# A decoder block in two halves of the sequence: the first half keeps both split parts of w_in in DRAM, the second half loads them

## The chip, the cores and the metric

The kernel runs on one core of one Trainium2 chip. The metric is device time in microseconds (us) from one execution of the whole program; lower is better. All arithmetic that counts is in float32: each operand of a large product is split into two parts, a rounded one ("hi", a type that TensorE multiplies in one pass) and the rest ("lo"), and a product is made of three matmuls, hi by hi, hi by lo and lo by hi.

## The reference

One layer (DEPTH is 1) on a sequence of 2048 positions, D_MODEL 1024.

```
h = rms_norm(x, mix_norm_pre)
z = h @ w_in                      # 1024 x 2560: q, k, v (512 each), xr, gr (512 each)
attn = dilated_attention(q, k, v) # 8 heads of 64, three dilations, mixed by their log-denominators
xr = causal_depthwise_conv(xr)    # 4 taps
rec = rg_lru(xr) * gelu(gr)       # h_t = a_t * h_(t-1) + u_t along the sequence
m = concat(attn, rec) @ w_out
x = x + rms_norm(m, mix_norm_post)
h = rms_norm(x, mlp_norm_pre)
x = x + rms_norm(square(relu(h @ w_ff_in)) @ w_ff_out, mlp_norm_post)
```

The change touches only how `w_in` reaches the matmuls of `z = h @ w_in`.

## The kernel before, in words

The sequence is worked on in two halves of 1024 positions (`hf` 0 and 1), each in two blocks of 512 (`b` 0 and 1). The columns of `w_in` are cut into 20 tiles of 128 (`ct` 0 to 19): 0 to 3 are q, 4 to 7 k, 8 to 11 v, 12 to 15 the recurrent input, 16 to 19 its gate. One tile is 8 slices of 128 by 128, 512 KB in all. `product` makes the projection of one tile and one block: 8 slices by 3 matmuls, 24 matmuls into one bank of PSUM, lines L198 to L200.

`load_w` brings a tile in. It loads the raw tile in two halves (`wraw`, 256 KB each, issued on the queue of the sync engine, SP), and `split` turns each half into `wH` (a cast on ScalarE, L54) and `wL` (a subtraction, L55). The subtraction runs on GpSimd (POOL in the profile) by default; for the first tiles, and after `pj.lo = nc.vector`, on VectorE (DVE). The pool has two buffers each for `wH`, `wL` and half a raw tile. All 20 tiles are loaded and split in the first half and once more in the second half. `load_ahead` calls `load_w` one step early.

The order of the work is a written list of steps. `ORDER` is "q00 r02 q01 a0 r03 q02 a1 q03 x2 x3 a2 q10 a3", then `BETWEEN` is "r10 r11 r12 r13" and `LATER` is "q11 q12 q13". A `q` step (half, pair of heads) projects q, k and v of a pair of heads and stores their split parts to scratch in DRAM (`sq`, `sk`, `sv`); an `r` step (half, group of 128 channels) does the projections 12+c and 16+c and the recurrence (`recurrent_block`); an `a` step is the attention of one pair of heads of the first half; `x` loads a block of 512 positions. Two recurrent groups of the first half run ahead of the list, in the pool `x0`. In one `r` step the four products stand in the order recurrent input of block 0, gate of block 0, recurrent input of block 1, gate of block 1. Inside this projection stage a scheduler sets the order of the instructions on every engine from their dependencies and a model of time; on SP, too, instructions are issued one after the other, and one that waits holds up those behind it.

After every step of the list some copies from the weights to a scratch in DRAM (`swo`, `sw`) are issued on POOL's own queue, eight at a time after an `r` step of the second half (L1552). In the last steps the loads of w_out (`woL`) and the first factors of the MLP weights (`er`, stored as `sf`) are added. From then on (output projection, MLP, attention of the second half, MLP again) `w_in` is not used.

## Time and profile before

| what | value |
|---|---|
| time, median of 3 runs | 2239.87 us (2238.17 to 2241.32) |
| the profiled execution: span from its first to its last instruction (the page gives no other time for it) | 2246.4 us |
| TensorE busy / weight loads busy | 2167.4 us (96%) / 1774.6 us (79%) |
| VectorE, ScalarE, GpSimd busy | 1506.9, 1230.9, 450.9 us |
| moved by DMA | 473.51 MB, mean 211 GB/s |
| splits of w_in, both halves: casts / subtractions on GpSimd / on VectorE | 81 / 58 / 23 |

The projection stage takes the first 640 us of the span, about 0 to 300 us for the first half's tiles and 300 to 640 us for the second half's. A busy share is the part of a stretch in which an engine had an instruction running; "PEclk" is the clock that TensorE was granted, as a part of full speed; the DMA share is the mean busy share of the 16 DMA engines. POOL's DMA instructions count in its busy time.

### The profile page before, as it was taken

Reading aid. Unit: us, or ns where it says so; the run is one execution under the profiler, and the core shown is the slowest. Engines: PE = TensorE matmul, PEld = TensorE weight load, DVE = VectorE, ACT = ScalarE, POOL = GpSimd, SP = SyncE. Lnnn points to the kernel's source line nnn. Section 1 sums busy time; section 2 is a strip of 40 time slices with the busy share of each in tenths; the row PEclk is TensorE's granted clock in tenths of the full one; section 3 lists DMA queues with packets and bytes.
Section 4 is the critical chain, followed back from the end, with each engine's and each line's share of the span. In section 5 each row is a group of like instructions: output and inputs, shape, how many; then the busy total and the mean of one; then the engine's idle time right before and its main releaser. Section 6 shows DMA issues by size and latency. Waiting matters only on the chain.

```text
span 2246.4 us, 30767 instructions
## 1 busy us (share of the span) xinstructions
PE 2167.4 (96%) x10264; PEld 1774.6 (79%) x10264; DVE 1506.9 (67%) x2908; ACT 1230.9 (55%) x2489; POOL 450.9 (20%) x536
## 2 busy tenths in 40 slices
PE   8999999979999999999999999989999999999998
PEld 6678878767788788888788787778878888888887
DVE  6767465978648867675567676777766566646456
ACT  7646464655434555554666666754455555654442
POOL 5543414455223000000001111113200000000003
PEclk9999999999999999999999999999999999999999
DMA  8365684645974676878777777877553444776665
GB/s 286 100 190 176 179 242 145 183 153 163 319 255 161 221 286 242 301 265 309 223 216 221 211 237 221 234 228 225 181 189 126 169 139 164 275 236 191 193 196 179
DMA packets 224116, 473.51 MB, mean 211 GB/s; under 512 B 23428, under 2 KB 78756, under 8 KB 217684
## 3 DMA queue, kind: packets, MB, share of 16 engines
q1 hardware_dynamic: 195140, 337.52, 47.9%
q0 software_dynamic: 28816, 134.01, 16.9%
q8 instruction: 81, 1.33, 0.2%
q14 instruction: 79, 0.65, 0.1%
HBM read 337.09 MB, written 151.13 MB: 217 GB/s over the span
## 4 chain that ended last, share of the span: by engine, by line
PE 70%; DVE 10%; DMA 8%; ACT 4%; issue 3%; POOL 1%; SPq 1%; DVEq 0%; ACTq 0%; POOLq 0%
PE o L1221 8%; PE o L1222 8%; PE o L1223 8%; PE za L1072 4%; PE za L1071 4%; PE za L1073 4%; PE z L198 3%; PE z L199 3%; PE z L200 3%; PE m L858 3%; PE m L857 3%; PE m L859 3%; PE zc L1071 2%; PE zc L1072 2%; PE zc L1073 2%
## 5 line engine op out<-in xcount | busy, mean ns | idle before, releaser
L198 PE MATMUL z<-hH,wH 128*128 128x512 f32 x640 | 263.8, 412 | 15.4 <-ACT wH L54 5.7
L199 PE MATMUL z<-hL,wH 128*128 128x512 f32 x640 | 260.5, 407 | 0.3 <-DVE hL L173 0.3
L200 PE MATMUL z<-hH,wL 128*128 128x512 f32 x640 | 259.6, 407 | 0.5 <-DVE wL L55 0.5
L198 PEld LDWEIGHTS z<-hH,wH 128*128 128x128 f32 x640 | 122.9, 192 | 50.6 <-ACT wH L54 8.3
L199 PEld LDWEIGHTS z<-hL,wH 128*128 128x128 f32 x640 | 122.8, 192 | 31.2 <-issue 4.8
L200 PEld LDWEIGHTS z<-hH,wL 128*128 128x128 f32 x640 | 122.9, 192 | 30.6 <-issue 4.6
L420 ACT ACTIVATE smB<-smB,stB 128x128 f32<-128x128 f32 (+3 forms) x128 | 71.6, 560 | 90.5 <-DVE stB L414 90.2
L1076 ACT ACTIVATE sq<-sq 128x512 f32<-128x512 f32 x93 | 58.8, 632 | 92.1 <-DVE sq L1080 92.1
L55 POOL TENSOR_TENSOR wL<-wraw,wH 128x512 fp32r<-128x512 f32 x58 | 82.4, 1437 | 80.5 <-ACT wH L54 76.7
L55 DVE TENSOR_TENSOR tlB<-pT_B,thB 128x384 fp32r<-128x384 f32 x96 | 57.1, 599 | 50.4 <-ACT thB L54 47.5
L1136 POOL DMA_DIRECT2D sa<-sq x31 | 16.6, 534 | 363.9 <-ACT sq L1077 353.4
L54 ACT CAST wH<-wraw 128x512 fp32r<-128x512 f32 (+1 forms) x81 | 47.2, 612 | 65.5 <-DMA wraw<-in_dram 31.6
L420 ACT ACTIVATE sm<-sm,stA 128x256 f32<-128x256 f32 (+1 forms) x128 | 63.1, 495 | 30.3 <-DVE stA L414 29.9
L1077 ACT ACTIVATE sq<-sq 128x512 f32<-128x512 f32 x124 | 76.2, 629 | 1.8
L1255 POOL TENSOR_TENSOR y<-y,g4b 128x512 f32<-128x512 f32 x8 | 12.3, 1577 | 259.4 <-ACT junk_y L84 259.4
L414 DVE CUSTOM_DVE_ANT_0 smB<-SB,mask_b 128x128 f32<-128x128 f32 (+3 forms) x128 | 59.3, 483 | 5.7 <-PE pT_B L393 5.4
L55 DVE TENSOR_TENSOR tlA<-pT,thA 128x512 fp32r<-128x512 f32 (+1 forms) x64 | 42.4, 670 | 26.4 <-ACT thA L54 26.0
L54 ACT CAST thB<-pT_B 128x384 fp32r<-128x384 f32 x96 | 48.4, 509 | 17.8 <-PE pT_B L393 9.7
L393 PE MATMUL pT_B<-ident,smB 128*128 128x128 f32 x320 | 51.5, 276 | 2.5 <-DVE na L409 0.9
L414 DVE CUSTOM_DVE_ANT_0 sm<-S,mask_a 128x256 f32<-128x256 f32 (+1 forms) x128 | 47.5, 410 | 9.3 <-PE pT L393 4.0
L640 PE MATMUL oB<-thB,vb 128*128 128x256 f32 x192 | 46.6, 274 | 6.6 <-ACT thB L54 5.9
L1072 PE MATMUL za<-hLT,f_5H 128*128 128x512 f32 x128 | 50.0, 391 | 2.0 <-DVE hLT L55 2.0
(607 smaller groups left out, 7041.4 us busy)
## 6 DMA issues: line engine op xcount, KB each, us to landing
sa<-as POOLq DMA_DIRECT2D x31, 1024.0 KB, 6.2
w1r<-in_dram SPq DMA_DIRECT2D x56, 512.0 KB, 4.0
sa<-sq POOLq DMA_DIRECT2D x31, 768.0 KB, 4.0
wraw<-in_dram SPq DMA_DIRECT2D x79, 256.0 KB, 3.8
place<-in_dram SPq DMA_DIRECT2D x14, 1024.0 KB, 7.9
sb<-place POOLq DMA_DIRECT2D x14, 1024.0 KB, 5.3
kh<-sk SPq DMA_DIRECT2D x24, 512.0 KB, 5.0
kl<-sk SPq DMA_DIRECT2D x24, 512.0 KB, 7.1
```

The lines of the kernel that those rows point to most:

```text
L55: (lo_eng or nc.vector).tensor_tensor(out=lo, in0=src, in1=f32(hi), op=ALU.subtract))
L198: pe.matmul(z, hi[:, k, :], hh, start=(k == 0), stop=False)
L199: pe.matmul(z, hi[:, k, :], hl, start=False, stop=False)
L200: pe.matmul(z, lo[:, k, :], hh, start=False, stop=(k == KT - 1))
L414: v.tensor_tensor_reduce(out=sm[:, c0:c0 + w], in0=sp[:, c0:c0 + w], in1=mask[:, mask.shape[-1] - w:], scale=1.0, scalar=3.0e38, op0=ALU.a ...
L420: s.activation(out=sm[:, c0:c0 + w], in_=sm[:, c0:c0 + w], func=AF.Exp, scale=-1.0, bias=st[:, 0, u, cols[j]:cols[j] + 1], accum_out=st[:, ...
L1071: pe.matmul(o, hi[:, k], bh[:, k], start=start and k == 0, stop=False, skip_group_check=True)
L1072: pe.matmul(o, hi[:, k], bl[:, k], start=False, stop=False, skip_group_check=True)
L1073: pe.matmul(o, lo[:, k], bh[:, k], start=False, stop=k == KH - 1, skip_group_check=True)
L1221: pe.matmul(o, ah[:, ts], bh, start=fresh and j == 0, stop=False, skip_group_check=True)
L1222: pe.matmul(o, ah[:, ts], bl, start=False, stop=False, skip_group_check=True)
L1223: pe.matmul(o, al[:, ts], bh, start=False, stop=j == NJ - 1, skip_group_check=True)
```

## The change

In the first half, each tile's `wH` and `wL` (512 KB each) are stored to a new scratch in DRAM (`swi`, 20 pairs) after the split, by SP's queue. In the second half `load_w` loads both parts from there straight into the buffers `wH` and `wL`; the raw loads, the casts and the subtractions of the second half are gone. The four tiles that were loaded ahead of the list (12, 16, 13, 17) are stored after the first group of recurrent blocks has been written in program order.

```diff
@@ load_w
         hi = p.tile([P, KT, P], F32R, tag="wH", bufs=4 if px else 2, name=f"wH{hf}_{ct}")
         lo = p.tile([P, KT, P], F32R, tag="wL", bufs=4 if px else 2, name=f"wL{hf}_{ct}")
+        if hf:
+            for d, t in zip(self.scr["wi"][ct], (hi, lo)):
+                nc.sync.dma_start(out=f32(t), in_=d)
+            return hi, lo
         for half in range(2):
             k0 = half * (KT // 2)
             raw = (px or self.pa).tile([P, KT // 2, P], F32, tag="wraw", bufs=6 if px else 2, name=f"wraw{hf}_{ct}_{half}")
             nc.sync.dma_start(out=raw, in_=self.w_in[ct, :, k0:k0 + KT // 2, :])
             split(nc, hi[:, k0:k0 + KT // 2, :], lo[:, k0:k0 + KT // 2, :], raw, lo_eng=lo_eng or self.lo)
+        if not px:
+            self.keep(ct, (hi, lo))
         return hi, lo
+
+    def keep(self, ct, w):
+
+        for d, t in zip(self.scr["wi"][ct], w):
+            self.nc.sync.dma_start(out=d, in_=f32(t))
@@ load_x
-            nc.scalar.activation(out=hi, in_=raw, func=AF.Identity, scale=self.g1[:, k:k + 1])
+            self.loaded = nc.scalar.activation(out=hi, in_=raw, func=AF.Identity, scale=self.g1[:, k:k + 1])
@@ trunk
+            "wi": [[d.tile([P, KT, P], F32, name=f"swi{ct}_{i}") for i in range(2)] for ct in range(20)],
...
                 pj.recurrent(0, (0, 1), w, px)
+                with tc.issue_after(pj.loaded.ins):
+                    for ct, t in w.items():
+                        pj.keep(ct, t)
                 pj.load_norm(2, px)
```

The scheduler makes a new order out of this. Two places of SP's queue and one of POOL's show it. In the names, the digit behind `wraw`, `wH`, `z` and the like is the half, and the next number the tile.

The queue of SP at the start, behind the loads of the second block of x (`xr1`), before:

```order
L167 DMA xr1_7_457<-in_1_dram 128x512
L110 DMA wraw0_0_0_915<-in_6_dram 128x512
L145 DMA xn1_0_464<-in_0_dram 128x1024
L110 DMA wraw0_0_1_919<-in_6_dram 128x512
L145 DMA xn1_1_467<-in_0_dram 128x1024
L145 DMA xn1_2_470<-in_0_dram 128x1024
L145 DMA xn1_3_473<-in_0_dram 128x1024
```

The same place with the change:

```order
L178 DMA xr1_7_497<-in_1_dram 128x512
L123 DMA swi12_0_233<-wH0_12_323 128x1024
L156 DMA xn1_0_504<-in_0_dram 128x1024
L123 DMA swi12_1_234<-wL0_12_324 128x1024
L123 DMA swi16_0_241<-wH0_16_385 128x1024
L156 DMA xn1_1_507<-in_0_dram 128x1024
L123 DMA swi16_1_242<-wL0_16_386 128x1024
L123 DMA swi13_0_235<-wH0_13_395 128x1024
L156 DMA xn1_2_510<-in_0_dram 128x1024
L123 DMA swi13_1_236<-wL0_13_396 128x1024
L114 DMA wraw0_0_0_963<-in_6_dram 128x512
```

Six stores of 512 KB now stand ahead of the raw tile 0 and between the loads of x for the norm of block 1 (`xn1`).

POOL, in the step r11 of the second half, before (`na`, `nb` close the attention of a pair of heads, `ge` is the gate's GELU, `smix` the stores of results):

```order
L55 TENSOR_TENSOR wL1_18_4948<-wraw1_18_0_4949,wH1_18_4947 128x512
L718 TENSOR_TENSOR na0_2_3357<-na0_2_3357,co0_2_0_3806 128x512
L55 TENSOR_TENSOR wL1_18_4948<-wraw1_18_1_4953,wH1_18_4947 128x512
L721 TENSOR_TENSOR nb0_2_3358<-nb0_2_3358,co0_2_0_3806 128x512
L307 TENSOR_SCALAR xc1_2_0_4986<-xr1_2_0_4982,cw_222,vec_cb_224 128x512
L338 TENSOR_TENSOR ge1_1_1_4921<-gr1_1_1_4919 128x512
L724 TENSOR_TENSOR na0_2_3357<-na0_2_3357,nb0_2_3358 128x512
```

The same place with the change:

```order
L318 TENSOR_SCALAR xc1_2_0_5012<-xr1_2_0_5008,cw_262,vec_cb_264 128x512
L349 TENSOR_TENSOR ge1_1_1_4959<-gr1_1_1_4957 128x512
L729 TENSOR_TENSOR na0_2_3431<-na0_2_3431,co0_2_0_3880 128x512
L350 TENSOR_SCALAR ge1_1_1_4959<-ge1_1_1_4959 128x512
L732 TENSOR_TENSOR nb0_2_3432<-nb0_2_3432,co0_2_0_3880 128x512
L351 TENSOR_TENSOR ge1_1_1_4959<-ge1_1_1_4959,gr1_1_1_4957 128x512
L735 TENSOR_TENSOR na0_2_3431<-na0_2_3431,nb0_2_3432 128x512
```

The subtractions are gone, and the recurrence's first tap (`xc`) and its gate move ahead of the attention's closing steps.

SP near the end of the stage, around the loads of w_out (`woL`), before:

```order
L110 DMA wraw1_6_0_5771<-in_6_dram 128x512
L110 DMA wraw1_6_1_5775<-in_6_dram 128x512
L792 DMA woL0_4_5374<-swo4_205 128x1024
...
L792 DMA woL0_3_5360<-swo3_204 128x1024
L244 DMA sv1_1_92<-vs1_9_0_5607 128x4x256
L1004 DMA er0_0_5657<-in_15_dram 128x512
...
L1004 DMA er0_3_5660<-in_15_dram 128x512
L110 DMA wraw1_10_0_5851<-in_6_dram 128x512
L110 DMA wraw1_10_1_5855<-in_6_dram 128x512
```

The same place with the change:

```order
L109 DMA wH1_10_5833<-swi10_0_229 128x1024
L109 DMA wL1_10_5834<-swi10_1_230 128x1024
L803 DMA woL0_4_5382<-swo4_205 128x1024
...
L803 DMA woL0_3_5368<-swo3_204 128x1024
L1015 DMA er0_0_5647<-in_15_dram 128x512
...
L1015 DMA er0_3_5650<-in_15_dram 128x512
L246 DMA sq1_2_77<-zh1_2_1_5751 64x512
L247 DMA sq1_2_77<-zl1_2_1_5752 64x512
L109 DMA wH1_3_5909<-swi3_0_215 128x1024
L109 DMA wL1_3_5910<-swi3_1_216 128x1024
```

Tile 10 now stands ahead of the eight loads of w_out and the four `er`, and tile 3 behind them; each tile is 1 MB instead of 512 KB.

## The prediction

> **What bounds the kernel now.** I read the page first (busy shares, the slices of the span, the chain that ended last), then the busy times by stage, then the waits and timelines in the stage where TensorE is not full.
>
> ```profile
> PE 2167.4 (96%) x10264; PEld 1774.6 (79%) x10264; DVE 1506.9 (67%) x2908; ACT 1230.9 (55%) x2489; POOL 450.9 (20%) x536
> PE   8999999979999999999999999989999999999998
> POOL 5543414455223000000001111113200000000003
> DMA  8365684645974676878777777877553444776665
> PE 70%; DVE 10%; DMA 8%; ACT 4%; issue 3%; POOL 1%; SPq 1%; DVEq 0%; ACTq 0%; POOLq 0%
> ```
>
> TensorE is busy 96% of the span, so whatever helps other engines can pay only where TensorE has gaps. A slice is 56 us; gaps show in the slices at 0, 450, 1630 and the end, and POOL works almost only in the first 13 slices, the projection stage that the change touches. By stage (the columns are start and end, length, busy us of each engine, granted clock, DMA share, GB/s):
>
> ```profile
> 0.00:285.00 285.00, 268.79 (x1268) 214.74 (x1269) 184.19 (x373) 168.84 (x329) 134.14 (x141) 0.98 0.61 188
> 285.00:345.00 60.00, 55.39 (x325) 47.56 (x324) 39.79 (x115) 37.61 (x99) 8.50 (x8) 0.94 0.78 234
> 345.00:415.00 70.00, 69.25 (x368) 57.42 (x367) 45.57 (x104) 40.08 (x96) 36.65 (x37) 1.00 0.60 184
> 415.00:520.00 105.00, 90.28 (x444) 69.62 (x443) 90.69 (x164) 62.27 (x125) 58.03 (x61) 0.95 0.40 126
> 520.00:560.00 40.00, 40.00 (x193) 31.67 (x192) 30.66 (x48) 17.99 (x28) 16.80 (x20) 1.00 0.64 200
> 560.00:640.00 80.00, 74.89 (x317) 59.73 (x316) 45.84 (x73) 31.49 (x56) 22.62 (x35) 0.96 0.95 316
> 640.00:2246.00 1606.00, 1568.76 (x7362) 1293.87 (x7360) 1070.20 (x2035) 872.58 (x1759) 174.12 (x239) 0.99 0.66 216
> ```
>
> After 640 us nothing changes but the order of a few instructions. In 415 to 520 (the last recurrent steps of the second half, with the last attention of the first half) TensorE misses 14.7 us of 105 and the clock is 0.95; there VectorE is busy 90.69 us and DMA only 0.40. In 560 to 640 (q12, q13, the loads of w_out) it is the reverse: TensorE misses 5.1 us, VectorE has room, DMA is at 0.95. The largest gap of the stage, on VectorE, GpSimd and TensorE:
>
> ```profile
> 463.99 7.32 DVE L331 TENSOR_TENSOR_SCAN xc<-r,state,i 128x512 f32<-128x512 f32 x1
> 464.09 1.28 POOL L721 TENSOR_TENSOR nb<-nb,co 128x512 f32<-128x512 f32 x1
> 465.31 1.27 POOL L340 TENSOR_TENSOR ge<-ge,gr 128x512 f32<-128x512 f32 x1
> 466.53 1.26 POOL L724 TENSOR_TENSOR na<-na,nb 128x512 f32<-128x512 f32 x1
> 467.75 2.47 POOL L55 TENSOR_TENSOR wL<-wraw,wH 128x512 fp32r<-128x512 f32 x2
> 472.10 2.05 PE L313 MATMUL pr<-xc,bd_r 128*128 128x512 f32 x2 [8.41 <-DVE state L332]
> 474.37 0.63 PE L199 MATMUL z<-hL,wH 128*128 128x512 f32 x1
> 477.64 0.40 PE L198 MATMUL z<-hH,wH 128*128 128x512 f32 x1
> 477.87 0.40 PE L199 MATMUL z<-hL,wH 128*128 128x512 f32 x1
> ```
>
> The scan of the recurrence ran 7.32 us while five GpSimd instructions ran one behind the other, two of them subtractions of w_in; TensorE waited 8.41 us and then ran cold until 477.6. This is no single case. By line in 415 to 520, and the least durations of the same lines over the whole run:
>
> ```profile
> L310 DVE SCALAR_TENSOR_TENSOR xc<-xr,cw,xc 128x512 f32<-128x512 f32 x16 | 16.0, 998 | 0.1
> L331 DVE TENSOR_TENSOR_SCAN xc<-r,state,i 128x512 f32<-128x512 f32 x5 | 12.4, 2480 | 0.0
> L305 DVE COPY tail<-xr 128x3 f32<-128x3 f32 x6 | 3.7, 609 | 0.1
> L303 DVE COPY xr<-tail 128x3 f32<-128x3 f32 x5 | 2.9, 587 | 0.1
> L310 DVE SCALAR_TENSOR_TENSOR xc<-xr,cw,xc x48: 720/752/3607, 41.0 to 521.7; 128x512 f32<-128x512 f32 x48
> L331 DVE TENSOR_TENSOR_SCAN xc<-r,state,i x16: 1264/1282/7320, 74.1 to 537.4; 128x512 f32<-128x512 f32 x16
> L305 DVE COPY tail<-xr x16: 145/170/1256, 39.9 to 517.1; 128x3 f32<-128x3 f32 x16
> L303 DVE COPY xr<-tail x16: 135/170/1329, 1.1 to 510.8; 128x3 f32<-128x3 f32 x16
> ```
>
> Mean less least, times count: 4.4 + 6.1 + 2.8 + 2.3 = 15.6 us of VectorE's 90.69 are stretch in these four lines.
>
> **The parts and their cost.**
>
> ```profile
> 415.00:520.00 105.00, 33.73 (x83) 15.89 (x82) 0.00 (x0) 14.88 (x10) 0.95 0.40 126
> by line: DVE xc L331 10.5%; issue 10.3%; DVE xc L310 7.6%; PE z L198 6.7%; PE z L199 5.7%; PE z L200 5.2%; DVE i L329 3.8%; DVE i L330 3.1%; POOL wL L55 2.5%; DVE ge L343 2.4%; ACT smB L420 2.4%; DVE tail L305 2.2%; DVE tlA L55 2.1%; DVE a
> wraw<-in_dram SPq DMA_DIRECT2D x14, 256.0 KB, 4.2
> woL<-swo SPq DMA_DIRECT2D x8, 512.0 KB, 7.3
> 585.11 0.50 PE L198 MATMUL z<-hH,wH 128*128 128x512 f32 x1 [2.02 <-DVE e_7L L1019]
> 586.37 0.55 PE L200 MATMUL z<-hH,wL 128*128 128x512 f32 x1 [0.53 <-DVE wL L55]
> 584.44 0.62 ACT L54 CAST wH<-wraw 128x512 fp32r<-128x512 f32 x1 [2.74 <-DMA wraw<-in_dram]
> ```
>
> The first row is the tile wL alone in 415 to 520 (GpSimd 14.88 us), the second the chain of waits inside 415 to 520 by line, the next two the loads in 520 to 640 (count, size, median us to landing), the last three the weight that came late at 585.
>
> 1. Subtractions gone, 415 to 520. In the scan above, wL is 2.47 of the 6.28 us of GpSimd beside it, 39%; that share of 15.6 is 6.1 us. Besides, wL itself stands on the chain with 2.5% of 105, 2.6 us. Together -8.7. Bounds: 0, if the attention's `na`, `nb` and the gates take its place beside the same VectorE lines (the order with the change puts them back to back), and -14.9, all of wL, if each subtraction had held VectorE for its whole length. I take -8.7, since the chain names both VectorE and wL there. The casts (all lie beside work; ScalarE is at 62 of 105) I cost at nothing; if ScalarE were late, the exponentials would be, which now wait for VectorE. The same subtractions in 345 to 415 cost TensorE nothing (69.25 of 70), nor does their removal give anything.
>
> 2. Loads straight into the buffers. With two buffers, the load of tile n+2 waits on SP for the last matmul of tile n; before, only the split did, and the raw tile was there. Behind that wait on SP stand the loads `vb`, `kh`, `qs` of the attention and the stores of the next tile's results; TensorE waits for the attention's, VectorE and ScalarE for the store buffers. In an `r` step one product of 24 matmuls (0.23 us apart by the rows at 477.64 and 477.87, 5.6 us) lies between the release and the need. To land 1 MB: 4.2 us as the median of the small load, plus 0.75 MB at 316 GB/s, 2.5, is 6.7; with woL's 7.3 for 512 KB, plus 0.5 MB, 1.7, it is 9.0. So 1.1 to 3.4 us late at each of eight handovers (r10 to q11), 9 to 27 us if nothing covered it. It is covered by the attention's matmuls that the scheduler puts between, and by VectorE, whose gaps TensorE has anyway. I take a quarter of a microsecond each, +2 (bounds 0 and +27; below nothing there is no reason for a gain).
>
> 3. The last stage, 520 to 640. 14 half tiles are 7 tiles, so 7 x 0.524 = 3.7 MB more, 11.6 us at 316 GB/s; DMA's spare time is 0.36 x 40 + 0.05 x 80 = 18.4 us, mostly ahead of the jam. Two gaps go the other way: at 585 TensorE waited 2.02 and 0.53 us for a weight that landed late behind w_out's loads and then for its subtraction in VectorE's queue; tile 10 now stands ahead of those loads. In a `q` step the cover is two products, 11.2 us. The spare 14.4 us before 560 can take two thirds of the 11.6 only if loads could run ahead, which two buffers allow for two tiles of seven; the queue slipping past 640 takes most of the rest. I leave +3.5 for later landings and take -2.5 for the gaps, net +1 (bounds -2.5 and +11.6). Late next would be tile 3, behind w_out and `er`, and the stores whose buffers `zh`, `zl` hold.
>
> 4. The stores, 40 x 524,288 bytes = 21 MB, 66 us at 316 GB/s; spare DMA time in 0 to 345 is 0.39 x 285 + 0.22 x 60 = 124 us, which hides them, unless they fall where x is loaded (285 to 345, where TensorE misses 4.6 us) or on the first 40 us. Six of them stand ahead of tile 0; tile 0 can wait, since TensorE now does block 1 of the four early tiles first. SP issues them between its other loads, and those of wL wait there for a subtraction, with loads of raw tiles behind. +0.5 (bounds -4.6, a lucky new order at 285, and +10).
>
> Sum: -8.7 + 2 + 1 + 0.5 = -5.2: the profiled execution would go from 2246.4 to 2241.2. Its span lies 6.5 us above the median of the runs, 2239.87; carried over, 2234.7.
>
> Weighed against the skill: the Trainium skill (SBUF — State Buffer, "Who interferes with whom") says that VectorE instructions with two SBUF inputs and GpSimd instructions share a port pair as an exclusive lock, and the later one stands still for the whole of the other. The trace agrees: 7.32 less 1.264 is 6.06, the five GpSimd pieces are 6.28. By that rule item 1 could reach its far bound, and the sum would be -11.4.
>
> **The rivals.**
>
> *Port relief in full*: every subtraction in 415 to 520 gave VectorE its whole length back, and the cold matmuls behind the gap (13 at 0.43 instead of 0.23, 2.6 us) go too: -14.9 - 2.6 + 3.5 = -14, 2226. For it speak the rows at 464; against it that three of those five instructions stay.
>
> *Handovers eat it*: the weights come 1.1 us late at each of eight handovers, the low end of item 2: -8.7 + 8.8 + 1.5 = +1.6, 2241.5, no change. For it: TensorE now has no raw tile in reserve, and the eight copies of an `r` step start just then. Against it: DMA at 0.40. The Trainium skill (DMA: Bandwidth & Descriptors, "Queues, rings and completion order") says that each DMA engine takes turns between queues packet by packet, so POOL's copies would share with SP's weights rather than wait behind them; no row here separates the two.
>
> *The jam at the end (slower)*: in 560 to 640 DMA is full, and the 11.6 us of extra transfers push the weights past the 11.2 us of two products: +11.6 there, -8.7 + 2 + 0.5 elsewhere, +5.4, 2245.3; with the same collision at 285 to 345 (+10) 2255. It decides from the point at which a 1 MB tile lands more than 11.2 us after its issue; `woL` has 7.3 for half of that. Against it: DMA work may slip past 640, where w_out and `place` are not yet needed.
>
> That the change doesn't do what it says is excluded by the order: no subtraction of the second half is left.
>
> **Numbers.** My forecast 0.33, full relief 0.10: faster 0.43. Handovers 0.21: same. The jam 0.24, and stores that delay x, the first norms or the first attention by 10 us (net +4 to +15) 0.12: slower 0.36. The bound is 0.2%, about 4.5 us, which is what a measurement here can tell from no change. The forecast's own range is 2229 to 2237; the range with the others reaches from full relief with a lucky 285 (2226 - 4) to the jam twice, 2255.
>
> **What would show it.** Right: in the recurrent steps of the second half the scan at L331 near 1.3 to 4 us, VectorE under 85 us and TensorE's gaps under 9 us in the stretch that is now 415 to 520; the rest of the span unchanged. Item 2 wrong: matmuls of z that wait for DMA wH or wL. Item 3 wrong: such waits after 560, or longer waits of `zh`, `zl` for the stores of `sq`. Item 4 wrong: more idle TensorE before 345. The forecast fails if those waits together exceed 9 us, or if the new order of the attention's closing steps meets the scans again.

## The result: 1.15% slower

The changed kernel took 2267.74 us (median; 2262.47 to 2271.91) beside 2239.02 us for the kernel before (2236.88 to 2241.32), a ratio of 1.0115 with a 95% interval of 1.0091 to 1.0139. The forecast was 2234.7 and its range ended at 2255. The profiled execution has a span of 2264.2 us, 3.5 below the median of its runs, while that of the kernel before lay 7.4 above its own: of the 28.7 us between the medians the two profiles show 17.8. So sizes below are taken from medians where a run gives them, and the profiles are read for where things happen. Among the runs of the experiments two single slow ones, 4562 us in e7 and 3033 us in e10, are left out of the ratios but not of the medians (without them 2239.4 and 2244.1).

First the page of the changed kernel: engines, slices, and the chain that ended last.

```profile
PE 2170.8 (96%) x10264; PEld 1776.1 (78%) x10264; DVE 1481.9 (65%) x2892; ACT 1213.6 (54%) x2451; POOL 415.5 (18%) x512
PE   8899989999969999999999999889999999999998
...
PE 68%; DMA 9%; DVE 7%; issue 3%; ACT 3%; POOL 2%; SPq 1%; DVEq 0%; POOLq 0%; ACTq 0%
```

VectorE lost 25 us of work, ScalarE 17, GpSimd 35, as the removal of the splits promised. TensorE's sum is nearly the same (2167.4 before), in a longer span. The stages, in the prediction's stretches:

```profile
0.00:285.00 285.00, 260.82 (x1193) 204.16 (x1194) 179.21 (x350) 163.06 (x305) 125.96 (x136) 0.98 0.74 248
285.00:345.00 60.00, 54.13 (x296) 46.90 (x295) 37.87 (x106) 37.19 (x97) 9.41 (x9) 0.91 0.83 262
415.00:520.00 105.00, 94.62 (x463) 73.71 (x462) 83.81 (x165) 60.87 (x120) 48.50 (x57) 0.98 0.57 191
560.00:640.00 80.00, 76.66 (x341) 61.55 (x339) 40.70 (x65) 23.70 (x42) 24.18 (x36) 1.00 0.89 307
640.00:2264.00 1624.00, 1574.63 (x7368) 1298.35 (x7368) 1068.63 (x2034) 875.79 (x1763) 176.49 (x241) 0.99 0.66 216
```

TensorE lost 8 us in the first 285 (260.82, before 268.79), gained 4.3 in 415 to 520 (94.62, before 90.28) and 1.8 in 560 to 640. Then it stood still right behind 640, where nothing was expected. The first output product, `m`, in the rows of its tile (count, least, median and most ns, first and last start), in the kernel before:

```profile
L857 PE MATMUL m<-woH,m_0H x64: 387/389/482, 637.4 to 727.0; 128*128 128x512 f32 x64
```

the same row of the changed kernel:

```profile
L868 PE MATMUL m<-woH,m_0H x64: 387/390/792, 652.8 to 750.1; 128*128 128x512 f32 x64
```

and what it waited for, in the waits of TensorE (total, times, longest):

```profile
PE m L868 <- ACT m_0H L54: 13.1, 1, 13.1
```

TensorE had ended the projection at the same time in both (the last `z<-hL,wH` starts at 636.5 before and at 636.2 after), so in the profiles the loss begins in the 13.1 us at that door. It goes on behind it: by the two rows of `m` the first starts 15.4 us later than before and the last of this half 23.1 later (750.1 for 727.0). The 20 us from 640 on show TensorE busy for 5.14 at a granted clock of 0.57:

```profile
640.00:660.00 20.00, 5.14 (x13) 3.32 (x13) 1.38 (x2) 2.44 (x4) 1.29 (x2) 0.57 1.02 318
```

SP's queue there in the changed kernel's timeline (start, length, line, transfer, count):

```profile
633.94 2.32 SPq L246 DMA_DIRECT2D sk<-zh  x2
636.36 3.78 SPq L859 DMA_DIRECT2D g2b<-in_dram  x2
642.01 3.19 SPq L247 DMA_DIRECT2D sk<-zl  x2
645.29 0.55 SPq L255 DMA_DIRECT2D sv<-vs  x1
645.93 1.89 SPq L246 DMA_DIRECT2D sk<-zh  x2
647.92 0.54 SPq L840 DMA_DIRECT2D m_0L<-smix  x1
```

and in the kernel before:

```profile
628.70 0.53 SPq L829 DMA_DIRECT2D m_0L<-smix  x1
630.80 1.08 SPq L235 DMA_DIRECT2D sq<-zh  x2
636.15 1.22 SPq L235 DMA_DIRECT2D sk<-zh  x2
```

The loads of the mix columns (`m_0L<-smix`) were issued at 628.7 before; now they stand behind the last key and value stores and the broadcasts `g2b`, and are issued at 647.9. ScalarE, which rounds the column, has the same stores ahead of it:

```profile
644.61 0.62 ACT L54 CAST zh<-zn 128x512 fp32r<-128x512 f32 x1 [6.73 <-DMA sk<-zh]
650.24 0.58 ACT L54 CAST vs<-vt 128x512 fp32r<-128x512 f32 x1 [5.01 <-DMA sv<-vs]
652.18 0.62 ACT L54 CAST m_0H<-m_0L 128x512 fp32r<-128x512 f32 x1 [1.36 <-DMA m_0L<-smix]
```

`zh` and `vs` wait for the store that still holds their buffer, and the column's cast comes third.

That the projection ended at the same time hides two things that cancel. A mark inside it is GpSimd's copy of `w_out`, of which each step of the first half issues one, the last behind q03 (the row's last number). Before:

```profile
L1552 POOL DMA_DIRECT2D swo<-in_dram x8: 509/520/570, 99.4 to 305.9; - x8
```

After:

```profile
L1567 POOL DMA_DIRECT2D swo<-in_dram x8: 507/516/567, 103.2 to 322.0; - x8
```

The first half ended 16 us later (322.0 for 305.9), and the second half took 16 us less (from there to the last `z`, 636.5 less 305.9 and 636.2 less 322.0: 330.6 before, 314.2 after). The experiments ask what each of the three is made of: the late first half, the faster second, the closed door at 640.

### The profile page after: what moved, and what is told of

Read it like the earlier page. It is cut to its first block, busy times and chain, and to the rows that moved or that the text cites. A ratio compares the mean times of both kernels' runs of the same rounds, so it can differ in the third digit from the quotient of the medians.

```text
span 2264.2 us, 30696 instructions
## 1 busy us (share of the span) xinstructions
PE 2170.8 (96%) x10264; PEld 1776.1 (78%) x10264; DVE 1481.9 (65%) x2892; ACT 1213.6 (54%) x2451; POOL 415.5 (18%) x512
## 4 chain that ended last, share of the span: by engine, by line
PE 68%; DMA 9%; DVE 7%; issue 3%; ACT 3%; POOL 2%; SPq 1%; DVEq 0%; POOLq 0%; ACTq 0%
PE o L1232 8%; PE o L1233 8%; PE o L1234 8%; PE za L1083 5%; PE za L1082 5%; PE za L1084 5%; PE zc L1084 2%; PE zc L1083 2%; PE zc L1082 2%; PE m L870 2%; PE m L868 2%; PE m L869 2%; PE z L209 2%; PE z L211 2%; PE z L210 2%
## 5 line engine op out<-in xcount | busy, mean ns | idle before, releaser
L868 PE MATMUL m<-woH,m_0H 128*128 128x512 f32 x128 | 52.2, 408 | 13.1 <-ACT m_0H L54 13.1
L1266 POOL TENSOR_TENSOR y<-y,g4b 128x512 f32<-128x512 f32 x8 | 12.4, 1577 | 259.3 <-ACT junk_y L84 259.3
L55 POOL TENSOR_TENSOR wL<-wraw,wH 128x512 fp32r<-128x512 f32 x34 | 45.8, 1360 | 38.7 <-ACT wH L54 32.2
L868 PE MATMUL m<-woH,m_4H 128*128 128x512 f32 x128 | 50.6, 396 | 1.9 <-ACT m_4H L54 1.9
L1082 PE MATMUL zc<-hHT,f_7H 128*128 128x512 f32 x128 | 50.7, 396 | 1.4 <-ACT hHT L54 1.4
```

What stands on the lines that cost most here:

```text
L55: (lo_eng or nc.vector).tensor_tensor(out=lo, in0=src, in1=f32(hi), op=ALU.subtract))
L868: pe.matmul(o, mh, wh[:, ds], start=(k == order[0]), stop=False)
L1082: pe.matmul(o, hi[:, k], bh[:, k], start=start and k == 0, stop=False, skip_group_check=True)
```

## The experiments

Three theories stood at the start. T1, a ledger: the stores cost some 10 us in the first half, the second half gives about as much back, and the late columns cost 15 or more. T2: the transfers themselves, 31 MB more, cost 25. T3: the stores are hidden. From e5 on an order theory (where an instruction stands, not what it moves) stands against T2. All eighteen runs; the mark behind q03, the last `z<-hL,wH` and the first `m` are the starts in the rows just shown, of each run's profile:

| run | median us | ratio to before, 95% | q03 mark | last z | first m |
|---|---|---|---|---|---|
| before | 2239.0 | | 305.9 | 636.5 | 637.4 |
| after | 2267.7 | 1.0115 (1.0091 to 1.0139) | 322.0 | 636.2 | 652.8 |
| e1 stores only | 2276.2 | 1.0156 (1.0135 to 1.0177) | 320.2 | 664.8 | 665.7 |
| e2 loads only | 2252.6 | 1.0055 (1.0034 to 1.0077) | 315.6 | 649.8 | 650.7 |
| e3 columns early | 2252.1 | 1.0054 (1.0036 to 1.0072) | 323.7 | 635.9 | 636.7 |
| e4 tiles 12 to 19 | 2245.5 | 1.0025 (1.0013 to 1.0038) | 314.6 | 637.5 | 638.4 |
| e5 one pair stored | 2246.3 | 1.0024 (1.0015 to 1.0033) | 316.4 | 641.4 | 642.2 |
| e6 stores by GpSimd | 2245.6 | 1.0024 (1.0007 to 1.0042) | 314.9 | 633.4 | 638.3 |
| e7 e4, tile 0 first | 2240.3 | 1.0007 (0.9992 to 1.0022) | 306.6 | 632.4 | 633.3 |
| e8 e2, dead subtractions | 2262.8 | 1.0102 (1.0085 to 1.0119) | 316.7 | 660.0 | 660.8 |
| e9 after, tile 0 first | 2263.4 | 1.0108 (1.0082 to 1.0134) | 320.8 | 632.8 | 650.1 |
| e10 e9, later stores by GpSimd | 2244.1 | 1.0020 (1.0005 to 1.0034) | 315.9 | 631.3 | 637.0 |
| e11 before, columns early | 2241.6 | 1.0010 (0.9994 to 1.0026) | 305.3 | 632.9 | 633.8 |
| e12 e7, later stores by GpSimd | 2238.7 | 1.0004 (0.9991 to 1.0016) | 307.0 | 633.0 | 633.9 |
| e13 e7, dead stores of q02, q03 | 2245.0 | 1.0027 (1.0013 to 1.0041) | 308.4 | 638.2 | 639.1 |
| e14 e10, dead subtractions | 2278.6 | 1.0172 (1.0156 to 1.0188) | 313.9 | 679.8 | 680.6 |
| e15 e7, q00, q01 stored and loaded | 2246.5 | 1.0023 (1.0013 to 1.0032) | 317.4 | 639.1 | 640.0 |
| e16 e15, later stores by GpSimd | 2248.6 | 1.0038 (1.0023 to 1.0052) | 314.8 | 637.1 | 638.0 |
| e17 e7, dead stores of q00, q01 | 2246.9 | 1.0036 (1.0023 to 1.0049) | 315.2 | 640.5 | 641.4 |
| e18 e17, an eighth of the bytes | 2246.9 | 1.0046 (1.0028 to 1.0063) | 314.0 | 637.7 | 638.6 |

How far two profiles of one order agree: e11 differs from the kernel before in nothing ahead of q13, and has 305.3 for 305.9 and 632.9 for 636.5. Differences of 4 us between profiles are not read. The table stops where the output product begins, and some runs lose time behind that: the last `m<-woH,m_0H` of the first half starts at 727.0 us in the kernel before, 729.0 in e11, 722.8 in e7, 750.1 in the changed kernel, 744.6 in e9, 737.1 in e3 and 727.2 in e10.

### The two parts of the change alone: e1, e2

e1 keeps all stores; the second half loads raw tiles and splits them:

```diff
-        if hf:
-            for d, t in zip(self.scr["wi"][ct], (hi, lo)):
-                nc.sync.dma_start(out=f32(t), in_=d)
-            return hi, lo
...
-        if not px:
+        if not px and not hf:
             self.keep(ct, (hi, lo))
```

> The changed kernel with the second half's loads undone: all 40 stores of the first half stay, the second half loads the raw tiles and splits them as before. Nothing reads the stored parts. Theory 1 (a ledger by stage, read from the two traces: the first half loses about 9 us to the stores, the recurrent steps of the second half gain about 11, the end of the projection stage loses 15 to 20 because the first columns for the output projection are loaded late): about +9 over the kernel before, 2248, with the step marks (copies issued on GpSimd after r10) some 9 us late and the first output product without a wait of over 3 us. Theory 2 (the extra bytes alone cost, wherever they fall: 31 MB for +25 us): 21 of 31 MB, +17, 2256. Theory 3 (stores are hidden, as predicted): 2239 to 2240.

Measured 2276.2: all three missed, by 20 us and more. The stores alone are worse than the whole change. What is more, half of what the profile shows up to the last `z` is lost where there is no store left (the last is issued at 290): the mark is 14.3 us late, and from the mark to the last `z` e1 takes 344.6 us, 14 more than the kernel before, with the same work. Its stretches 415 to 520 and 520 to 560:

```profile
415.00:520.00 105.00, 90.03 (x418) 67.99 (x417) 85.28 (x172) 61.77 (x134) 52.23 (x55) 0.90 0.49 162
520.00:560.00 40.00, 37.57 (x182) 29.23 (x181) 31.32 (x50) 20.58 (x33) 20.90 (x23) 0.96 0.39 128
```

DMA has half its time free there, so it is no matter of bytes; TensorE has gaps and a clock of 0.90 (0.95 before).

e2 stores the pair of tile 12 alone, and every tile of the second half loads that pair:

```diff
-            for d, t in zip(self.scr["wi"][ct], (hi, lo)):
+            for d, t in zip(self.scr["wi"][12], (hi, lo)):
...
-        if not px:
-            self.keep(ct, (hi, lo))
...
-                    for ct, t in w.items():
+                    for ct, t in [(12, w[12])]:
```

> The changed kernel with the first half's stores left out but for one tile: the second half loads both parts of each tile from the one stored pair (so all tiles of the second half get tile 12's values; the bytes and the instructions are the same). Theory 1: the gain of the recurrent steps without the cost of the stores, -11 or so; the first columns of the output projection stand ahead of the key stores on SP's queue in this order, so the end loses 0 to 5: 2228 to 2234. Theory 2: 10 of 31 MB, +8, 2247. Predicted by the sum on record: -5.7, 2233.

Measured 2252.6, slower than every theory had it. With 1 MB stored instead of 21 the mark still came at 315.6. That gave the order theory. The second half is slow too: from the mark to the last `z` e2 takes 334.2 us, more than the kernel before, though every split of that half is gone. Between 320 and 660 TensorE waits 17.9 us in it for loaded weights (10.5 for `wH`, 7.4 for `wL`; the changed kernel waits 6.1).

### The door at 640: e3, e11

e3 is the changed kernel with the loads of two mix columns written ahead of q13 instead of behind it; e11 is the same edit on the kernel before:

```diff
+            ready = []
             for step in LATER.split():
                 run(step)
...
+                if step == "q13":
+                    ready = [mix_columns(nc, sh, scr, 0, order, t) for t in range(2)]
...
-            ready = [mix_columns(nc, sh, scr, 0, order, t) for t in range(2)]
```

(In the file the new lines stand ahead of `run(step)`.)

> The changed kernel whole, with the loads of the first two columns of the output projection written ahead of the step q13, so that they stand ahead of the key stores on SP's queue. Same bytes, same splits. Theory 1: the 13 us wait of the first output product and the cold matmuls behind it go, 2267.7 becomes 2248 to 2253; what stays above before is the stores' cost less the recurrent gain. Theory 2 (the DMA engines are simply full at the end, so something else waits): 2260 or more.

> Control: the kernel before with e3's edit, the loads of the first two mix columns written ahead of q13. In the kernel before they already stand ahead of the last key stores, so nothing should be gained: 2237 to 2242 (each theory). If the edit were a gain of its own, whatever the change, 2225 to 2232, and e3 would say nothing on the change.

e3 took 2252.1, 15.6 less than the changed kernel, and its first `m` starts at 636.7, behind the last `z` without a gap; up to there TensorE's instructions stand in the same order in both profiles. e11 changed nothing that can be measured (1.0010, 0.9994 to 1.0026). So the place of these loads in SP's queue is 15.6 of the 28.7 us, and only because the change moved it. T2's 2260 or more is refuted: the bytes are all there.

The door is not all open in e3. Its page still has one long wait for a column (busy, mean ns, idle before and what ended it):

```profile
L868 PE MATMUL m<-woH,m_0H 128*128 128x512 f32 x128 | 52.1, 407 | 7.3 <-ACT m_0H L54 7.3
```

It ends at 666.5 us, at a column behind the two that were moved. The load of that column is issued at 657.1, behind the last key and value stores, the broadcasts `g2b` and `g3b` and the loads `xt`. No run moves this one alone.

### The late first half: e4 to e7, e9, e10, e12

e4 stores and loads the eight tiles 12 to 19 only, those of the recurrent steps:

```diff
-        if hf:
+        if hf and ct >= 12:
...
-        if not px:
+        if not px and not hf and ct >= 12:
```

> The change for the eight tiles of the recurrent part alone (12 to 19): these are stored and loaded, the twelve tiles of q, k and v are loaded raw and split in both halves as before. 8.4 MB of stores, 4.2 MB more of loads. Theory 1: stores 8/20 of 9, +4, recurrent gain -11, end as before: about 2232. Theory 2: 12.6 of 31 MB, +10, 2249. If the gain of the recurrent steps is not from the subtractions taken off GpSimd but from a lucky order: 2239 or more.

2245.5, between T1's 2232 and T2's 2249: the mark at 314.6, and 0.25% slower where item 1 of the prediction alone should have given a gain. e5 tests whether the first half is late because anything at all stands ahead of tile 0: the kernel before, with one pair stored (`keep`, `swi` and `loaded` as in the change):

```diff
+                with tc.issue_after(pj.loaded.ins):
+                    for ct, t in [(12, w[12])]:
+                        pj.keep(ct, t)
```

> Before, with one addition: the two parts of tile 12 alone (1 MB instead of 21 MB) are stored where the change stores the six early tiles ahead of tile 0; the second half loads and splits as before. Order theory (the first stage loses its 10 us because any wait put ahead of tile 0's load makes TensorE do the four early tiles' second block first, and everything behind it stands in another order): the mark behind r03 at 255 to 258 instead of 248, the one behind q03 at 313 to 318 instead of 306, time 2245 to 2252. Bytes theory (the stores' transfers crowd x and the first attention out): 1 MB is 3.3 us of DMA in a stage with 124 us spare, marks and time of the kernel before, 2238 to 2241.

2246.3, mark 316.4: as the order theory said. Two transfers of 512 KB, issued at 24.5 and 25.8 us, with the order that the scheduler made around them, cost 7.8 us. e7 puts tile 0's load ahead of the early stores of e4. (These are the pairs of the four early tiles, eight stores; the texts on record speak of the six of them that the change puts ahead of tile 0.)

```diff
+                pj.load_ahead(0, 0)
                 with tc.issue_after(pj.loaded.ins):
```

> e4 (only the eight tiles 12 to 19 are stored and loaded) with one line more: tile 0's load is written ahead of the six early stores, so that TensorE gets tile 0 as early as in the kernel before. If the late tile 0 is what loses the first stage's 10 us: the mark behind r03 at 247 to 250, time 2233 to 2240. If the loss lies in the later order (attention and recurrence meet on VectorE, whatever tile 0 does): marks as in e4 (254, 315), time 2243 to 2248. Bytes theory: as e4, 2245.

Mark 306.6, time 2240.3, 5.3 less than e4: for these eight tiles the whole loss of the first half goes with the late tile 0. e6 leaves the changed kernel as it is, but issues the stores from GpSimd's queue:

```diff
-            self.nc.sync.dma_start(out=d, in_=f32(t))
+            self.nc.gpsimd.dma_start(out=d, in_=f32(t))
```

> The changed kernel with all 40 stores of w_in's parts issued by GpSimd's queue instead of SP's; bytes unchanged. This order has the first mix columns ahead of the last key stores, as e3 had by hand. Order theory: the first half loses its 10 us all the same (a store still waits and still takes the DMA engines, and tile 0 still comes late), nothing is lost at 640: 2246 to 2253, the mark behind q03 at 313 to 324. Queue theory (what costs is SP's own queue, in which the loads stand behind stores that wait for a subtraction): the mark behind q03 back at 304 to 308, time 2230 to 2240. Bytes theory: as e3, 2252 or more, the marks of e3.

2245.6 at the same bytes, 6.5 less than e3, which also has its first columns early, but still the wait of 7.3 us behind them, which e6 has not (the intervals, 1.0007 to 1.0042 and 1.0036 to 1.0072, just overlap). The mark is 9 earlier than in e3, yet not back: the order theory's time was just missed, its mark hit. Next the same first line of e7 on the changed kernel (e9), and with all but the early stores on GpSimd's queue (e10); e12 is e7 in this form.

```diff
-    def keep(self, ct, w):
+    def keep(self, ct, w, e):
...
-            self.nc.sync.dma_start(out=d, in_=f32(t))
+            e.dma_start(out=d, in_=f32(t))
...
-            self.keep(ct, (hi, lo))
+            self.keep(ct, (hi, lo), nc.gpsimd)
...
+                pj.load_ahead(0, 0)
...
-                        pj.keep(ct, t)
+                        pj.keep(ct, t, nc.sync)
```

> The changed kernel with tile 0's load written ahead of the six early stores (all 40 stores still on SP's queue; the mix columns' loads stand behind the last key stores as in the changed kernel). Ledger (the late tile 0 costs 8 to 10 us in the first half, the other stores on SP's queue 6 to 7, the late columns at 640 some 15; the recurrent steps give back 16): the mark behind q03 at 313 to 316 instead of 322, the wait of 10 to 13 us at the first output product still there, time 2256 to 2263. If the first half's delay was absorbed later in any case: 2265 to 2270.

> The changed kernel with all its stores and loads, tile 0's load ahead of the six early stores, and the other stores issued by GpSimd's queue; this order has the mix columns ahead of the last key stores. Ledger (the change's own gain is the 8 to 10 us of the recurrent steps, and its losses are three places of order and queue, all of which this removes): the mark behind q03 at 304 to 308, no wait at the first output product, time 2228 to 2237, faster than the kernel before. Bytes theory (42 MB more must cost 10 us or more): 2248 or more. Luck (the second half's order decides by 10 us either way): 2237 to 2247.

> e7 (tiles 12 to 19 alone are stored and loaded, tile 0's load ahead) with the two stores pairs that are not early issued by GpSimd's queue, the six early ones by SP's. Ledger: the queue's share of eight tiles is small, marks as in e7 (306.6), 2234 to 2241. Luck: 2240 to 2248.

e9 took 2263.4, hardly below the changed kernel (the intervals lie on one another), and its mark stayed at 320.8: with 40 stores the early tile 0 does not save the first half. It still waits 12.4 us for `m_0H`. e10 took 2244.1, so all 31 MB more (by the pages; the 42 in the text on record is too many) can go at 5.7 us over the kernel before, but the ledger's 2228 to 2237 failed. Its mark, 315.9, is late as well, but its last `z` at 631.3 is not; the first `m` starts 5.7 us behind that, and between them the transposes of v wait for VectorE (1.3 and 2.4 us). No run says which of these is the 5.7 us of its time. e12 equals e7 and the kernel before.

### Which stores, and whether their bytes: e13, e15 to e18

e7 has a good first half, e10 not; between them lie the stores of the q tiles. e13 adds those of q02 and q03 to e7, e17 those of q00 and q01, read by nobody; e15 stores and also loads q00's and q01's; e16 is e15 with the later stores on GpSimd's queue as in e10. The condition in `load_w`, in e13, then e17; and e15's for the loads:

```diff
-        if not px and not hf and ct >= 12:
+        if not px and not hf and (ct >= 12 or ct % 4 > 1):
...
+        if not px and not hf and (ct >= 12 or ct % 4 < 2):
...
-        if hf and ct >= 12:
+        if hf and (ct >= 12 or ct % 4 < 2):
```

> e7 (tiles 12 to 19 stored and loaded, tile 0's load ahead) with the pairs of the six tiles of q02 and q03 stored as well, and read by nobody: 6 MB more, between 200 and 290 us. If these stores' transfers delay the small ones of the first half's attention: the loads and stores of sco and smix between 250 and 290 land in 6 to 9 us instead of 3 to 5, the mark behind q03 at 312 to 317 instead of 306.6, time 2245 to 2252. If they are hidden, and e10's late first half is a matter of its order: the mark at 305 to 309, time 2237 to 2243.

> e7 with the pairs of q00's and q01's tiles stored and loaded besides those of tiles 12 to 19, all on SP's queue; the tiles of q02 and q03 are not stored, so that q12 and q13 load raw tiles and split them. If the stores of q02 and q03 are what costs in the first half, and the loads of q10 and q11 give some of what the changed kernel gains over e7 in the second: the mark behind q03 at 305 to 310, last product of z at 622 to 630, time 2228 to 2236, faster than both kernels. If each q tile's store costs alike: the mark at 311 to 314, time 2238 to 2244.

> e15 with all but the six early stores issued by GpSimd's queue. If SP's queue has no part in the loss: as e15 within 4 us. If it has: 3 to 6 us faster than e15.

> e7 (tiles 12 to 19 stored and loaded, tile 0's load ahead) with the pairs of the six tiles of q00 and q01 stored as well, and read by nobody. As in e15 the mark behind q03 should come at 313 to 318 instead of e7's 306.6 (every theory, since e15 had these stores too); time 2244 to 2252.

e13's expectation of a late mark fell: with q02's and q03's stores the mark is 308.4, that is, they are hidden up to there (the run is 4.7 us slower than e7 all the same; the profile puts that in the second half, last `z` 638.2, and no run says why). It is q00's and q01's stores that make the first half late, 317.4, 314.8 and 315.2, on either queue. e15's mark lies beyond both of its expectations, and e15 and e16, meant as versions that beat both kernels, are slower than the one before. e18 sets bytes against place: e17 with an eighth of the bytes in these twelve stores.

```diff
-            self.nc.sync.dma_start(out=d, in_=f32(t))
+            n = KT if ct >= 12 else 1
+            self.nc.sync.dma_start(out=d[:, :n, :], in_=f32(t)[:, :n, :])
```

> e17 with one eighth of the bytes in the stores of q00's and q01's tiles (64 KB each instead of 512), at the same places of SP's queue. If these stores cost as transfers: the mark behind q03 back at 305 to 309, time 2238 to 2243. If they cost because SP's queue waits at them for the split, and the loads behind stand still: the mark at 313 to 318 and the time of e17.

The same time, 2246.9, and nearly the same mark, 314.0 for 315.2. So these transfers show no cost, and the twelve instructions do; the intervals (1.0023 to 1.0049 and 1.0028 to 1.0063) would hide a few us. The two have not quite one order: in the profiles some rows of SP's queue and of TensorE stand in other places in e18 than in e17. TensorE's order in e18 is nearly that of e7 in the first 2300 matmuls, so the difference was looked for in SP's queue. Its waits between 80 and 345 us (who waited for whom, total, times, longest) in e7:

```profile
SPq L123 <- ACT wH L54: 14.6, 3, 7.4
```

and in e18:

```profile
SPq L124 <- ACT wH L54: 22.5, 4, 10.4
```

but in e17, which is as late as e18:

```profile
SPq L123 <- ACT wH L54: 13.3, 4, 9.9
```

A store of `wH` waits for its cast and holds up everything that stands behind it. SP's queue near the first of these places, in e7's timeline:

```profile
100.33 0.33 SPq L123 DMA_DIRECT2D swi<-wH  x1
106.66 0.33 SPq L114 DMA_DIRECT2D wraw<-in_dram  x1
108.74 0.42 SPq L114 DMA_DIRECT2D wraw<-in_dram  x1
116.80 0.83 SPq L512 DMA_DIRECT2D va<-sv  x2
```

and in e18's:

```profile
111.35 0.33 SPq L124 DMA_DIRECT2D swi<-wH  x1
112.22 0.33 SPq L114 DMA_DIRECT2D wraw<-in_dram  x1
114.30 0.42 SPq L114 DMA_DIRECT2D wraw<-in_dram  x1
124.88 2.43 SPq L513 DMA_DIRECT2D va<-sv  x4
```

The raw tile behind the store comes 5.6 us later (112.2 for 106.7), the attention's first `va` 8.1 later; the mark behind r02, which in e7 stands at 125.5, stands at 136.6 in e18. That this wait is the cause isn't shown, and two runs speak against it: e17 has no more of it in all than e7 (13.3 for 14.6 us), and e16 has these stores on GpSimd's queue, keeps e12's mark behind r02 (126.9 for 126.6) and loses the same 8 us later.

### Where the second half's gain comes from: e8, e14

Both put GpSimd's work back, as subtractions whose result nobody reads: e8 into e2, e14 into e10.

```diff
+            if self.lo is nc.gpsimd:
+                for half in range(2):
+                    raw = self.pa.tile([P, KT // 2, P], F32, tag="wraw", bufs=2, name=f"dead{hf}_{ct}_{half}")
+                    ks = slice(half * (KT // 2), (half + 1) * (KT // 2))
+                    nc.gpsimd.tensor_tensor(out=raw, in0=f32(hi[:, ks, :]), in1=f32(lo[:, ks, :]), op=ALU.subtract)
             return hi, lo
```

> e2 (every tile of the second half loads the stored pair of tile 12, so its values are not the reference's) with a subtraction on GpSimd added for each half tile of the recurrent steps, whose result nobody reads: GpSimd's work is back, the loads and splits stay away. Contention theory (item 1 of the prediction): the scan of the recurrence goes from 1.4 back to 2 us or more on average, VectorE in 415 to 540 busy 5 to 10 us more, time 2258 to 2264 against 2252.6. If the gain came from the loads and casts that went (raw tiles, ScalarE), not from GpSimd: 2250 to 2255, scans at 1.4.

> e10 (all stores and loads, tile 0 ahead, the later stores on GpSimd's queue) with a subtraction on GpSimd for each half tile of q10 and the recurrent steps of the second half, whose result nobody reads: GpSimd's work is back as in the kernel before. Item 1 (the subtractions hold VectorE and stand on the chain of the recurrent steps): 8 to 12 us slower than e10, 2252 to 2257, as e8 was 10 us slower than e2. If the gain comes from the casts, the raw loads or the q tiles: within 3 us of e10, 2242 to 2247.

e8 was 10.2 us slower than e2, e14 34.5 slower than e10. That is more than item 1 said, and not for its reason alone. The recurrence's lines in 415 to 540, in e10:

```profile
L321 DVE SCALAR_TENSOR_TENSOR xc<-xr,cw,xc 128x512 f32<-128x512 f32 x18 | 14.7, 816 | 0.1
L342 DVE TENSOR_TENSOR_SCAN xc<-r,state,i 128x512 f32<-128x512 f32 x7 | 11.3, 1613 | 0.1
```

and in e14:

```profile
L326 DVE SCALAR_TENSOR_TENSOR xc<-xr,cw,xc 128x512 f32<-128x512 f32 x15 | 20.1, 1342 | 2.6 <-POOL xc L323 2.5
L347 DVE TENSOR_TENSOR_SCAN xc<-r,state,i 128x512 f32<-128x512 f32 x6 | 8.9, 1479 | 0.1
```

TensorE's longest wait for weights between 345 and 660, in e10:

```profile
PE z L211 <- DMA wL<-swi: 3.6, 4, 1.7
```

and in e14:

```profile
PE z L216 <- DMA wL<-swi: 13.9, 5, 5.8
```

The convolution stretched, 1342 ns for 816; the scan did not, and e8's expectation of 2 us failed too (1500). And TensorE waited 13.9 us for `wL` where e10 had 3.6. It would fit that a subtraction which reads both parts holds their two buffers, and with them the next load, but the profile does not show it: SP's loads in e14 wait for TensorE's matmuls (75.0 us in 8 waits), and no wait of theirs ends with GpSimd. So these two runs don't isolate the price of GpSimd's work.

The runs without it are these. From the mark to the last `z`, where the first half is not late: 330.6 (before), 327.6 (e11), 325.8 (e7), 326.0 (e12), 329.8 (e13). None of the second half's splits removed and the first half late: 325.0 (e5). With tiles 12 to 19 loaded: 322.9 (e4), 325.3 (e17), 323.7 (e18). With q10's and q11's tiles as well: 321.7 (e15), 322.3 (e16). With all: 314.2 (after), 312.2 (e3), 318.5 (e6), 312.0 (e9), 315.4 (e10). By these the recurrent steps' tiles give at most 2 us, which profiles can't tell from nothing, and the loads of the q tiles, those of q12 and q13 above all, some 9. Against so neat a reading stand e1, which removes nothing either and takes 344.6, and e2, which removes all and takes 334.2: an order can throw this stretch further than the work in it, so where the changed kernel's 16 us come from is not shown.

## Why the prediction was wrong, point by point

Two steps failed above all: item 3 let the queue slip past 640 us as if nothing there were waiting, and item 4 priced the stores by their bytes.

**Item 1, the subtractions (-8.7).** The mechanism is there, the size is not. In 415 to 520:

```profile
L321 DVE SCALAR_TENSOR_TENSOR xc<-xr,cw,xc 128x512 f32<-128x512 f32 x18 | 15.7, 874 | 2.2 <-POOL xc L318 2.1
L342 DVE TENSOR_TENSOR_SCAN xc<-r,state,i 128x512 f32<-128x512 f32 x5 | 7.2, 1438 | 0.0
```

The scan fell from 2480 to 1438 ns, the convolution from 998 to 874, VectorE by 6.9 us and TensorE's idle time by 4.3. But e7 and e12, which do this for the recurrent steps, with 16 stores and 16 direct loads beside it, are as fast as the kernel before; in them the relief is smaller, too (in e7, 415 to 540, the scan falls from 2138 to 1448 ns and the convolution rises from 970 to 1080). e7 in 415 to 520 and in 560 to 640:

```profile
415.00:520.00 105.00, 94.47 (x469) 73.69 (x467) 93.63 (x169) 63.83 (x126) 53.31 (x62) 0.96 0.49 171
560.00:640.00 80.00, 74.02 (x323) 59.20 (x322) 43.99 (x71) 29.50 (x53) 20.52 (x32) 0.98 0.92 298
```

It gains 4.2 us of TensorE in the first and gives 0.9 back in the second; its time does not move. The failing step is the one that took VectorE's stretch as the kernel's time: of 8.7 us TensorE got 4.3 in the stretch, and no run's time shows any, which is the bound 0, as far as runs with their own stores and loads can say. The rule of the Trainium skill (SBUF — State Buffer, "Who interferes with whom") by which this item could have reached -14.9 is borne out in the stretch of single instructions (the scan's 2480 ns beside GpSimd's subtractions, 1438 without) and not in the time of any run here. What it says of a lock for the whole instruction it says of VectorE's two-port modes; of an instruction with two SBUF inputs, like the scan, it says that it contends with a GpSimd instruction that reads SBUF.

**Item 2, the direct loads (+2).** Late weights cost TensorE 6.1 us between 300 and 660:

```profile
PE z L209 <- DMA wH<-swi: 4.2, 3, 2.2
PE z L211 <- DMA wL<-swi: 1.9, 3, 0.8
```

That is inside the bounds and three times the value taken. The two parts landed in 4.3 and 5.6 us, medians from the issue of each; the estimate of 6.7 was for the pair, which no row gives. The rival in which the handovers eat the gain (8.8) was the nearer one here, and in e2, with 17.9 us, even that was passed.

**Item 3, the last stage (+1).** Right that the weights would not be late: with 3.7 MB more TensorE gained 1.8 us in 560 to 640, and DMA fell from 0.95 to 0.89. Wrong by 15.6 us, measured by e3, because of the sentence that the queue may slip past 640, "where w_out and `place` are not yet needed": the mix columns are, and they stand in the same queue (so is w_out: the first `m`, at 637.4 before, multiplies `woH`). "After 640 us nothing changes but the order of a few instructions" was the mistake in small: the order was what mattered. The stores that hold `zh` and `zl` were named as late next, and were:

```profile
DVE zl L55 <- DMA sk<-zl: 15.1, 2, 9.9
```

The rival of the jam at the end had the side and, with its 2245 to 2255, the nearest time, but not the mechanism: it turned on a 1 MB tile landing more than 11.2 us after its issue, and TensorE waited only 0.8 us for loaded weights after 520.

**Item 4, the stores (+0.5).** The main error besides item 3. It set 21 MB against 124 us of spare DMA time, and no run contradicts that part: an eighth of the bytes in twelve of the stores changed nothing that can be measured (e18). But it priced the transfers and not the instructions. Two stores ahead of tile 0 cost 7.8 us (e5), twelve in q00 and q01 6.7 more on a kernel whose tile 0 was early (e17 against e7), and the whole set, with the second half's old work in a new order, 36 (e1). The sentence "tile 0 can wait, since TensorE now does block 1 of the four early tiles first" had the fact and drew the wrong price from it; that loads stand behind a store that waits for a subtraction was written down and given nothing. The rival with the late x, norms and first attention (+4 to +15) is the one that happened in the first half, where the mark came 16 us late.

**The sum.** Of 28.7 us, 15.6 are the first two columns (e3). From e3 to e10 it is 8.0 more, for tile 0, the queue of the later stores and the order that came of them together. That is not simply the first half: at the first `m` the two stand level (636.7 and 637.0), and they part behind it (last `m` at 737.1 and 727.2), where e3 has its wait of 7.3 us for a later column and e10 has none. So the columns may have cost more than 15.6, and the stores' place less than 8.0; no run separates them. 5.1 remain in e10 (5.7 beside the runs of its own call), with whatever the second half gained already taken off. No version ran faster than the kernel before.

**Open.** Which single wait of the first half carries the 8 us of e17 and e18; why e1 needs 20 us more than e5 from the mark to the last `z`, with the same instructions in it; why TensorE waits 17.9 us for weights in e2 and 6.1 in the changed kernel; and how much of e14's 34.5 is GpSimd's contention. But for e3, where two columns' loads moved, an order of instructions was never changed alone, with all else held, so that "order" is what is left when bytes (e18) and work (e5, e13) are excluded, not one shown chain.

## What to carry to other kernels

Here the added transfers cost by where they stood, and no cost of their bytes was seen: ask what a transfer waits for, what stands behind it in its queue, and which load it pushes back, before setting its megabytes against spare DMA time. Where a scheduler writes the order, one added pair of stores can move the whole stage by 8 us, so read the new order at the far end of the kernel too, at the first instruction of the next stage and at its loads. And an engine's stretched time becomes the kernel's time only where a run with that edit alone says so.

## What the runs showed of the hardware

Twelve stores of 64 KB cost the kernel what twelve of 512 KB did, as far as the intervals can tell (2246.9 us both, e18 and e17). Issued from GpSimd, the same stores occupy that engine longer than SP (least, median and most ns of one). e6:

```profile
L123 POOL DMA_DIRECT2D swi<-wH x20: 531/577/630, 11.3 to 287.9; - x20
```

The changed kernel:

```profile
L123 SPq DMA_DIRECT2D swi<-wH x20: 325/356/1097, 25.7 to 286.3; - x20
```

Even so the kernel was 6.5 us faster with them there than in SP's queue (e6 against e3); what of that is the queue and what the order that came with it, e3's wait of 7.3 us behind 640 above all, was not taken apart. And a reader that nobody needs is not free: with the dead subtractions on GpSimd TensorE waited 10 us more for `wL` (13.9 us in e14, 3.6 in e10), by which way is open.
